# A seven-product MLP with one ring for its operands, some inner features stored in two parts, and transposes between its steps

## Chip, cores, metric

The kernel runs on one core of a Trainium2 chip. The metric is the device time of one execution in microseconds. Lower is better. Engines: TensorE (PE), VectorE (DVE), ScalarE (ACT), GpSimd (POOL) and SyncE (SP), which here only issues transfers. Transfers are also issued from ACT's and POOL's queues.

## The reference

Two blocks over 1024 tokens of width 1024, in float32. The first mixes by pooling, sparse attention and a short convolution, adds to the residual, and ends with a gated MLP; the second has spatial gating, window attention and attention to a memory of 256 rows. What matters here:

```
h  = h + m @ w_o
hn = rms_norm(h, norm2_g)
gate, up = split(hn @ w_gate_up)            # 1024 -> 2 x 2816
h  = h + (silu(gate) * up) @ w_down         # 2816 -> 1024
x  = rms_norm(h, final_g)                   # then the second block:
mkv = rms_norm(mem, mem_norm_g) @ w_mem_kv  # needs mem alone
bias = rel_bias[buckets]                    # a table for the window attention
```

## The kernel before

Every float32 product is made from three products of parts: an operand is split into hi (rounded, by an ACT copy) and lo (the rest, by a subtraction on POOL or DVE), and `mm3` (L283 to L285) issues hi x hi, hi x lo and lo x hi. So each operand costs two splits before TensorE can use it. Engines run their instructions in the order of the program text, each its own queue; `Side` objects insert small pieces of other work as TensorE advances (`tick` counts TensorE time, a generator yields the price of each piece).

The stages that the change touches, in order of time:

- **wb** (878 to 997 us). `proj_t` multiplies attention output by w_b, 16 outputs of 24 matmuls, each worth 8 x 0.64 us of ticks. For each output POOL issues loads of `g1d` and `mpart` (`load_gp`, L1062, L1063, two pairs of buffers), DVE multiplies and adds (L1078, L1079), ACT copies the hi part to `mh` (L1080), POOL subtracts the lo part. Two sides run: `mem_steps` (load a row of memory on POOL's queue, sum of squares, norm, transposes; two rows of tiles through one buffer) and `bias_steps` (32 small operations on POOL into `G`, then a transfer that writes `G`, 4 partitions x 384, 128 times each into the DRAM tile `gd`, issued from POOL).
- **wo** (997 to 1130 us). `mem_kv` (two passes of 48 matmuls), then the residual rows: `add_rows` for four column groups j of w_o and eight row tiles t. For j = 2 and 3 the loop goes over t: rows j = 2, rows j = 3, transposes of tile t - 2 (`first_turns`), and `norm2(t)`: two sums of squares on ACT, stores to `hres` on SP, reciprocal root and scaling on DVE, and for t >= 4 two differences of half tiles, one on POOL and one on DVE.
- **mlp** (1130 to 1605 us). The 2x2 block products are made with seven multiplications instead of eight. `gu_seq` lists the steps: a unit is 128-wide gate or up columns of a pair, seven products p each; a step is `gu_mm` (four `mm3` of 512 columns) and `gu_out` (eviction and block sums). For the first two units the products come in another order, because the transposed operands `TM[p]` are still being made by `turns(p)` (`turn4`: four transposes into one of two `ax` banks, ACT copies hi, DVE subtracts lo). `gu_prep` splits the weights of a step up to six steps ahead into `wpart` tiles (a ring of 8). After each pair `hidden_sums` makes four sums on POOL and seven 256 KB stores to `hd` follow behind the next `gu_mm`. `hb` tiles are a ring of 19.
- **down** (1605 to 1845 us). 77 steps m (seven products x 11 pairs): `dn_load` (one or two pieces of w_down into `rb`, one of `hd` into `ra`, rings of 8), `dn_sum`, `dn_hi` (two ACT copies), `dn_lo` (two DVE subtractions), then four `mm3`. `dn_ahead(m)` runs loads 7, sums 4, hi 3 and lo 2 steps ahead. The pool of these tiles opens when the pool of `TM[3..7]` closes, after the last `gu_mm`. The residual `h` is read back by eight 512 KB loads on ACT's queue at the start. The last products run beside `final_steps` (norms of finished tiles).

## Time and profile before

| what | value |
|---|---|
| median of three runs | 2282.96 us (2282.51, 2282.96, 2289.36) |
| profiled execution | 2287.99 us, span 2286.2 us |
| PE busy | 2178.9 us, 95% |
| PEld busy | 1879.6 us, 82% |
| DVE busy | 1349.0 us, 59% |
| POOL busy | 835.4 us, 37% |
| ACT busy | 786.4 us, 34% |
| granted TensorE clock, mean | 0.982 |
| DMA | 210.54 MB, 92 GB/s |

TensorE is busy nearly all the time, so what is to be read is where it is not: its waits, and the windows in which its clock is below full. A matmul's duration in a row is longer than its distance from the next one, because matmuls are pipelined; prices are taken from counts in a window of known length.

### The profile page before, as it was taken

To read this page: it belongs to the slowest core of one execution; us is meant where nothing else is said; L and a number is where in the kernel's file an instruction comes from. 1 tells how busy PE (TensorE), PEld (TensorE's weight loads), DVE (VectorE), ACT (ScalarE), POOL (GpSimd) and SP (SyncE) were. 2 spreads that over 40 slices of the span, in tenths; PEclk is the share of its full clock that TensorE was granted. 3 is DMA by queue.
4 is the path that set the end of the run, shared out by engine and by line. 5 is a ranking of instruction groups with operands and counts; after the bars stand their busy time and mean duration, and the time that the engine had idled before them with its cause. 6 is when DMAs were issued, how large, how long until landed. Compare 5 with 4: busy or idle time off the path is not lost. (4 is left out here: it accounts for less than half of the span.)

```text
span 2286.2 us, 31336 instructions
## 1 busy us (share of the span) xinstructions
PE 2178.9 (95%) x11855; PEld 1879.6 (82%) x11855; DVE 1349.0 (59%) x2712; ACT 786.4 (34%) x1548; POOL 835.4 (37%) x714
## 2 busy tenths in 40 slices
PE   7999999999999998969879999999799999999998
PEld 7789889998888887759858888888588789987998
DVE  6688998888892886411745333333477760831724
ACT  4573211121123875211233323222344532322631
POOL 1213322224533212633138777685100112671121
PEclk9999999999999999989989999999899999999999
DMA  4212222113321001335202323231976422120013
GB/s 144 70 65 75 65 74 65 56 38 111 115 70 38 1 1 56 121 82 167 97 26 87 114 92 116 92 116 51 341 280 207 171 75 70 47 65 19 1 62 142
DMA packets 144359, 210.54 MB, mean 92 GB/s; under 512 B 14768, under 2 KB 93332, under 8 KB 144208
## 3 DMA queue, kind: packets, MB, share of 16 engines
q1 hardware_dynamic: 127120, 162.55, 21.5%
q0 software_dynamic: 8800, 27.54, 3.5%
q10 hardware_dynamic: 8288, 18.45, 2.1%
q8 instruction: 93, 1.52, 0.3%
q14 instruction: 58, 0.48, 0.1%
HBM read 161.80 MB, written 46.66 MB: 91 GB/s over the span
## 5 line engine op out<-in xcount | busy, mean ns | idle before, releaser
L97 POOL TENSOR_TENSOR wpart<-wraw,wpart 128x1024 fp32r<-128x1024 f32 (+1 forms) x108 | 261.6, 2442 | 532.9 <-ACT wpart L96 531.2
L285 PE MATMUL mm<-xh,wpart 128*128 128x512 f32 (+2 forms) x736 | 269.9, 367 | 0.0
L284 PE MATMUL mm<-xl,wpart 128*128 128x512 f32 (+2 forms) x736 | 269.5, 366 | 0.0
L283 PE MATMUL mm<-xh,wpart 128*128 128x512 f32 (+2 forms) x736 | 269.0, 365 | 0.0
L608 DVE MAX8 m<-scores 128x8 f32<-128x272 f32 (+6 forms) x224 | 188.8, 843 | 6.4 <-POOL scores L570 0.2
L610 DVE MATCH_REPLACE8 scores<-m,scores 128x272 f32<-128x272 f32 (+6 forms) x224 | 184.9, 826 | 0.0
L285 PE MATMUL mm<-th,wpart 128*128 128x512 f32 x440 | 175.9, 400 | 6.5 <-POOL wpart L312 6.5
L283 PE MATMUL mm<-th,wpart 128*128 128x512 f32 x440 | 175.5, 399 | 3.8 <-ACT wpart L1226 3.8
L284 PE MATMUL mm<-tl,wpart 128*128 128x512 f32 x440 | 175.2, 398 | 0.0
L96 ACT ACTIVATE wpart<-wraw 128x1024 fp32r<-128x1024 f32 (+1 forms) x110 | 111.5, 1048 | 151.4 <-issue 80.5
L284 PEld LDWEIGHTS mm<-xl,wpart 128*128 128x128 f32 x736 | 138.5, 188 | 20.5
L283 PEld LDWEIGHTS mm<-xh,wpart 128*128 128x128 f32 x736 | 138.3, 188 | 20.3
L285 PEld LDWEIGHTS mm<-xh,wpart 128*128 128x128 f32 x736 | 138.3, 188 | 19.6
L283 PE MATMUL mm<-wpart,hh 128*128 128x256 f32 x512 | 142.7, 279 | 1.3 <-ACT ev L1717 1.3
L284 PE MATMUL mm<-wpart,hh 128*128 128x256 f32 x512 | 142.5, 278 | 0.0
L285 PE MATMUL mm<-wpart,hl 128*128 128x256 f32 x512 | 142.3, 278 | 0.0
L312 POOL TENSOR_TENSOR wpart<-hb,wpart 128x512 fp32r<-128x512 f32 x88 | 116.7, 1330 | 60.3 <-ACT wpart L1226 39.2
L283 PE MATMUL mm<-wpart,pa 128*128 128x512 f32 x242 | 97.0, 401 | 15.1 <-ACT pa L1417 15.1
L285 PEld LDWEIGHTS mm<-th,wpart 128*128 128x128 f32 x440 | 83.6, 190 | 27.8 <-POOL wpart L312 7.8
L283 PEld LDWEIGHTS mm<-th,wpart 128*128 128x128 f32 x440 | 83.4, 189 | 24.6 <-ACT wpart L1226 5.1
L284 PE MATMUL mm<-wpart,pa 128*128 128x512 f32 x242 | 97.6, 403 | 5.5 <-DVE wpart L312 5.5
L284 PEld LDWEIGHTS mm<-tl,wpart 128*128 128x128 f32 x440 | 83.4, 190 | 20.1
(382 smaller groups left out, 5716.4 us busy)
## 6 DMA issues: line engine op xcount, KB each, us to landing
wraw<-in_w_in_dram SPq DMA_DIRECT2D x68, 512.0 KB, 3.6
rb<-in_w_down_dram SPq DMA_DIRECT2D x99, 256.0 KB, 5.4
wraw<-in_w_gate_up_dram SPq DMA_DIRECT2D x44, 512.0 KB, 4.1
hd<-hb SPq DMA_DIRECT2D x77, 256.0 KB, 2.0
ra<-hd SPq DMA_DIRECT2D x77, 256.0 KB, 4.8
mpart<-ev POOLq DMA_DIRECT2D x32, 256.0 KB, 2.3
ev<-mpart POOLq DMA_DIRECT2D x32, 256.0 KB, 4.0
xr<-in_x_dram SPq DMA_DIRECT2D x8, 512.0 KB, 5.9
```

Source lines behind the costliest of these rows:

```text
L96: nc.scalar.activation(hi[:, :nk * w], r, AF.Copy)
L97: (low or nc.gpsimd).tensor_tensor(lo[:, :nk * w], r, hi[:, :nk * w].bitcast(F32), op=ALU.subtract)
L283: nc.tensor.matmul(o, sh, mh, start=start, stop=False, skip_group_check=more)
L284: nc.tensor.matmul(o, sh, ml, start=False, stop=False, skip_group_check=more)
L285: nc.tensor.matmul(o, sl, mh, start=False, stop=stop, skip_group_check=more)
L312: (eng or nc.gpsimd).tensor_tensor(out_lo, src, hi.bitcast(F32), op=ALU.subtract)
L608: nc.vector.max(m8, s)
L610: nc.vector.match_replace(out=s, in_to_replace=m8, in_values=s, imm_value=TAKEN)
```

## The change

The diff changes five places:

1. `bias_steps` yields less per step and 8 more at its end, and issues the `gd` transfer from ACT. `mem_steps` yields 30 (first) and 10 (second) after its row's load instead of 8.
2. `norm2` becomes `norm2_a` (sums of squares, stores) and `norm2_b` (the rest); the loop over t runs rows j = 2 of tile t + 1 ahead of `norm2_b(t - 1)` and rows j = 3 of tile t. `gu_sums(0)`, the first preps and the load of unit 1 move up in that loop.
3. `TM[3..7]` take ten tiles of one ring `tm`, whose slots the down steps use afterwards: a pair of steps takes one tile for `rb` and one for `pa`. The ring stays open through down, so a load may start when its slot's `TM` is no longer read. Loads run 8 steps ahead. For products with two weight pieces, `ra` is half a `wraw` tile. `h` is loaded in 16 pieces of 256 KB at the odd steps up to 7 of the first four products.
4. For products p = 4, 6 and 3 the inner features are stored as hi and lo parts (`SPLIT`): one more ACT copy and DVE subtraction in mlp, a second 256 KB store, 512 KB instead of 256 KB to load, and one split less in down. Stores are spread over the four steps after a pair.
5. The first units run in another order: each `mm3` of the first six steps is followed by one `turn4`. `W.ahead` at the end of down is emitted three steps earlier.

```diff
-                yield 1.5
-        nc.gpsimd.dma_start(gd, G.unsqueeze(1).to_broadcast([4, 128, 384]))
+                yield 1.2
+        yield 8.0
+        nc.scalar.dma_start(gd, G.unsqueeze(1).to_broadcast([4, 128, 384]))
...
-            yield 8.0
+            yield 30.0 if r == 0 else 10.0
...
+    add_rows(mh, ml, wo[2], 0, 2)
     for t in range(NT):
-        add_rows(mh, ml, wo[2], t, 2)
-        if t == 6:
-            gu_sums(0)
-        if t == 7:
-            for n in range(3):
-                gu_prep(n)
+        if t + 1 < NT:
+            add_rows(mh, ml, wo[2], t + 1, 2)
+        if t:
+            norm2_b(t - 1)
         add_rows(mh, ml, wo[3], t, 3)
+        if t < 7:
+            norm2_a(t)
         if 2 <= t < 6:
             first_turns(t - 2)
-        norm2(t)
+        if t == 4:
+            gu_sums(0)
+        if t == 6:
+            gu_prep(0)
+            gu_prep(1)
+            gu_load(1)
+        if t == 7:
+            gu_prep(2)
+    norm2_a(7)
...
+    def tm_tile():
+        return tmp_.tile([128, 2048], F32R, name="tm", bufs=10)
...
+    SPLIT = (4, 6, 3)
...
     def store(p, pr, t):
-        later.append(lambda: nc.sync.dma_start(hd[p - 1, pr], t))
+        if p not in SPLIT:
+            nc.sync.dma_start(hd[p - 1, pr, :, :512], t)
+            return
+        hi = hb_tile().bitcast(F32R)
+        nc.scalar.activation(hi, t, AF.Copy)
+        lo_of(t.bitcast(F32R), t, hi, nc.vector)
+        nc.sync.dma_start(hd[p - 1, pr, :, :512], hi.bitcast(F32))
+        nc.sync.dma_start(hd[p - 1, pr, :, 512:], t)
...
-        for p, t in ((1, a11), (2, a12), (4, a22), (7, s3), (5, a21), (6, s2), (3, s4)):
-            store(p, pr, t)
+        for k, (p, t) in enumerate(((1, a11), (2, a12), (4, a22), (7, s3), (5, a21), (6, s2),
+                                    (3, s4))):
+            at(n + 1 + k // 2, lambda p=p, t=t: store(p, pr, t))
...
             mm3(o, hi[:, k, :], lo[:, k, :], th[:, k, :], tl[:, k, :], first and k == 0, k == 3, not first)
-        for f in later:
-            f()
-        later.clear()
+            if extra:
+                turns(*extra.pop(0))
...
+        if m % 2 == 0:
+            DN["rb"], DN["pa"] = tm_tile(), tm_tile()
+            DN["ra"] = None
+        rb, pa = (DN[k][:, 1024 * (m % 2):1024 * (m % 2) + 1024] for k in ("rb", "pa"))
+        ra = rb[:, 512:]
+        if len(parts) == 2:
+            if DN["ra"] is None:
+                DN["ra"] = W.raw_tile()
+            ra = DN["ra"][:, 512 * (m % 2):512 * (m % 2) + 512].bitcast(F32R)
...
+        if p in SPLIT:
+            nc.sync.dma_start(pa.bitcast(F32), hd[p - 1, i])
+        else:
+            nc.sync.dma_start(ra.bitcast(F32), hd[p - 1, i, :, :512])
...
-        dn_load(m + 7)
+        dn_load(m + 8)
         dn_sum(m + 4)
         dn_hi(m + 3)
         dn_lo(m + 2)
...
+    norm2_b(7)
     gu_prep(3)
+    gu_prep(4)
+    gu_mm(0, [(5, t) for t in range(3)])
+    gu_out(0)
+    gu_mm(1, [(3, t) for t in range(3)])
+    sums24(range(3))
+    gu_sums(1)
+    gu_prep(5)
+    gu_mm(2, [(7, 0), (7, 1), (7, 2), (5, 3)])
+    gu_out(2)
+    gu_mm(3, [(3, 3), (7, 3), (6, 0), (6, 1)])
+    sums24((3,))
+    gu_out(1)
+    gu_out(3)
     gu_prep(6)
     gu_prep(7)
+    gu_mm(4, [(6, 2), (4, 0), (4, 1), (4, 2)])
+    gu_out(4)
+    gu_prep(8)
+    gu_prep(9)
+    gu_mm(5, [(6, 3), (4, 3)])
+    gu_out(5)
...
-    close(tmp_)
     dn_open()
     for n in (last - 1, last):
         gu_out(n)
-    for f in later:
-        f()
-    later.clear()
+    run_todo(last + 9)
...
-    for t in (4, 5, 6, 7, 0, 1, 2, 3):
-        nc.scalar.dma_start(h[:, t, :], hres[t])
+    h_load = [(t, c) for ts, c in ((range(4, 8), 1), (range(4), 0), (range(4, 8), 0), (range(4), 1))
+              for t in ts]
...
+        if i in (1, 3, 5, 7) and h_load:
+            t, c = h_load.pop(0)
+            nc.scalar.dma_start(h[:, t, 512 * c:512 * c + 512], hres[t, :, 512 * c:512 * c + 512])
+        if p == 3 and i == NPAIR - TAIL - 1:
+            W.ahead()
```

## Rows read from the trace of the kernel before

**Rows 1.** The page, part 2: TensorE's granted clock in tenths, 40 slices
```profile
PEclk9999999999999999989989999999899999999999
```

**Rows 2.** Windows: length, busy PE PEld DVE ACT POOL (xcount), clock, DMA share, GB/s
```profile
980.00:1000.00 20.00, 17.78 (x77) 13.94 (x75) 0.00 (x0) 0.00 (x0) 0.00 (x0) 1.00 0.24 26
1060.00:1080.00 20.00, 20.00 (x172) 20.00 (x172) 2.97 (x7) 0.01 (x1) 3.30 (x2) 1.00 0.17 54
1240.00:1260.00 20.00, 20.00 (x88) 16.13 (x87) 11.80 (x13) 5.21 (x9) 16.88 (x13) 1.00 0.31 105
1660.00:1680.00 20.00, 20.00 (x89) 16.43 (x88) 14.49 (x24) 8.40 (x15) 0.00 (x0) 1.00 1.04 382
```

**Rows 3.** Timeline of PE, transposes: start us, us, engine, line, operation, count
```profile
1152.06 1.03 PE L1145 MATMUL ax<-ident,hb 128*128 128x128 f32 x8
```

**Rows 4.** Waits of PE, whole span: us in total, times, longest us
```profile
PE mm L283 <- ACT wpart L96: 16.5, 2, 9.5
PE mm L283 <- ACT pa L1417: 15.1, 2, 10.8
PE mm L285 <- POOL wpart L312: 11.2, 4, 5.2
...
PE mm L1044 <- DVE mrow L1038: 9.4, 2, 8.9
```

**Rows 5.** Windows round the five stretches, columns as in rows 2
```profile
909.00:931.00 22.00, 13.15 (x50) 10.33 (x49) 9.04 (x24) 5.81 (x13) 9.92 (x21) 0.77 0.42 148
997.00:1036.10 39.10, 18.02 (x101) 16.75 (x100) 6.79 (x10) 9.87 (x14) 24.46 (x17) 0.69 0.37 123
1130.40:1200.30 69.90, 47.79 (x191) 35.06 (x189) 33.99 (x58) 23.18 (x43) 26.35 (x18) 0.83 0.15 48
1605.00:1632.00 27.00, 11.85 (x43) 8.67 (x42) 8.36 (x11) 5.84 (x11) 8.54 (x6) 0.79 0.95 352
1805.50:1845.40 39.90, 34.06 (x134) 25.37 (x134) 35.37 (x58) 17.80 (x32) 10.39 (x4) 0.96 0.26 92
```

**Rows 6.** Timelines of POOL, DVE and ACT at the end of wb
```profile
967.77 1.14 POOL L1026 DMA_DIRECT2D gd<-G  x1 [0.30 <-POOL G L1022]
...
1001.68 0.69 DVE L1078 TENSOR_TENSOR ev<-mm,ev 128x512 f32<-128x512 f32 x1 [30.39 <-DMA ev<-g1d]
...
1022.10 0.69 DVE L1078 TENSOR_TENSOR ev<-mm,ev 128x512 f32<-128x512 f32 x1 [4.09 <-DMA ev<-g1d]
...
1024.22 1.99 ACT L96 ACTIVATE wpart<-wraw 128x1024 fp32r<-128x1024 f32 x2
...
1025.62 9.36 POOL L97 TENSOR_TENSOR wpart<-wraw,wpart 128x1024 fp32r<-128x1024 f32 x4
```

**Rows 7.** DMA issues: count, KB each, median us from issue to landing
```profile
gd<-G POOLq DMA_DIRECT2D x1, 768.0 KB, 33.2
```

**Rows 8.** Timeline of DVE at the start of mlp
```profile
1137.17 0.74 DVE L1139 TENSOR_TENSOR hb<-mm,hb 128x256 f32<-128x256 f32 x2
...
1144.17 0.69 DVE L1173 TENSOR_TENSOR hb<-hb 128x512 f32<-128x512 f32 x1 [1.17 <-POOL hb L1172]
...
1158.57 4.67 DVE L1449 TENSOR_TENSOR hb<-hb 128x512 f32<-128x512 f32 x4
```

**Rows 9.** Timelines of SP, ACT and POOL between mlp and down
```profile
1605.74 0.33 SPq L1386 DMA_DIRECT2D rb<-in_w_down_dram  x1
...
1612.96 16.75 ACTq L1495 DMA_DIRECT2D hh<-hres  x8
...
1613.70 3.01 POOL L1291 TENSOR_TENSOR hb<-ev,hb 128x512 f32<-128x512 f32 x2 [11.47 <-DVE ev L1290]
...
1621.21 1.26 POOL L1303 TENSOR_TENSOR hb<-hb 128x512 f32<-128x512 f32 x1
```

**Rows 10.** Timeline of DVE at the end of down
```profile
1823.31 1.28 DVE L329 SCALAR_TENSOR_TENSOR hh<-hh,ry,pg 128x1024 f32<-128x1024 f32 x1
...
1829.31 3.42 DVE L329 SCALAR_TENSOR_TENSOR hh<-hh,ry,pg 128x1024 f32<-128x1024 f32 x1
```

More of the change, by code (lines that the diff above doesn't have):

```diff
@@ L1158, in build, with norm2_a, norm2_b @@
     TM = {}
-    def norm2(t):
-        ss = [work.tile([128, 4], F32, name="ss", bufs=4)[:, :1] for _ in range(2)]
+    ssq = {}
+    def norm2_a(t):
+        ssq[t] = [work.tile([128, 4], F32, name="ss", bufs=4)[:, :1] for _ in range(2)]
         for c in range(2):
-            sumsq(ht[t, c], ss[c])
+            sumsq(ht[t, c], ssq[t][c])
             nc.sync.dma_start(hres[t, :, 512 * c:512 * c + 512], ht[t, c])
-        nc.vector.tensor_tensor(ss[0], ss[0], ss[1], op=ALU.add)
-        y = rstd_b(rstd_a(ss[0]))
+    def norm2_b(t):
+        s0, s1 = ssq.pop(t)
+        nc.vector.tensor_tensor(s0, s0, s1, op=ALU.add)
+        y = rstd_b(rstd_a(s0))
         for c in range(2):
@@ L1337, in gu_out @@
             if u:
-                hidden_sums(u)
+                hidden_sums(u, n)
         elif p == 6:
@@ L1364, in gu_step, with turns @@
         gu_out(n)
-    def turns(p, ts=range(4)):
-        for t in ts:
-            turn4(ht[{5: (t, 0), 7: (t + 4, 0), 3: (t + 4, 1), 6: (t + 4, 1), 4: (t, 1)}[p]],
-                  *TM[p], 128 * t)
+    def turns(p, t):
+        turn4(ht[{5: (t, 0), 7: (t + 4, 0), 3: (t + 4, 1), 6: (t + 4, 1), 4: (t, 1)}[p]],
+              *TM[p], 128 * t)
     DN = {}
@@ L1414, in dn_hi @@
             return
-        dn_ops[m] = (W.part_tile(), DN["p"].tile([128, 1024], F32R, name="pa", bufs=6))
-        for o, src in zip(dn_ops[m], dn_src(m)):
-            nc.scalar.activation(o[:, :512], src, AF.Copy)
+        dn_ops[m] = W.part_tile()
+        nc.scalar.activation(dn_ops[m][:, :512], dn_src(m), AF.Copy)
+        if dn_seq[m][0] not in SPLIT:
+            rb, ra, pa = dn_raw[m]
+            nc.scalar.activation(pa[:, :512], ra.bitcast(F32), AF.Copy)
     def dn_lo(m):
@@ L1421, in dn_lo @@
             return
-        for o, src in zip(dn_ops[m], dn_src(m)):
-            lo_of(o[:, 512:], src, o[:, :512], nc.vector)
+        lo_of(dn_ops[m][:, 512:], dn_src(m), dn_ops[m][:, :512], nc.vector)
+        if dn_seq[m][0] not in SPLIT:
+            rb, ra, pa = dn_raw[m]
+            lo_of(pa[:, 512:], ra.bitcast(F32), pa[:, :512], nc.vector)
     def dn_ahead(m):
-        dn_load(m + 7)
+        dn_load(m + 8)
         dn_sum(m + 4)
@@ L1432, in dn_open @@
     def dn_open():
-        DN["p"] = pool("dn", side="left")
-        for m in range(7):
+        for m in range(8):
             dn_load(m)
@@ L1439, in dn_open, with sums24 @@
                 dn_lo(m)
[L1441 to L1451 removed]
+    def sums24(ts):
+        for t in ts:
+            nc.vector.tensor_tensor(ht[t + 4, 1], ht[t + 4, 1], ht[t, 0], op=ALU.subtract)
+            nc.gpsimd.tensor_tensor(ht[t, 1], ht[t, 1], ht[t + 4, 1], op=ALU.subtract)
+    norm2_b(7)
+    gu_prep(3)
+    gu_prep(4)
[9 more added lines that the diff above has]
+    sums24((3,))
     gu_out(1)
     gu_out(3)
[L1454 to L1459 removed]
     gu_prep(6)
     gu_prep(7)
[L1462 to L1469 removed]
+    gu_mm(4, [(6, 2), (4, 0), (4, 1), (4, 2)])
[4 more added lines that the diff above has]
+    gu_out(5)
+    ahead = 10
     last = len(gu_seq) - 1
[L1471 removed]
+    for n in range(6, last - 1):
         while ahead <= min(n + 6, last):
@@ L1574, in build @@
                     dn_ops.pop(g)
+                    dn_raw.pop(g)
             if len(grp) > 1:
@@ L1581, in build @@
     fa = Side(final_steps(range(4)))
-    W.ahead()
     MARK("fin")
     close(ttp)
-    close(DN["p"])
+    close(tmp_)
     yp = pool("y", side="left")
```

67 lines of the change are left out of this document (23 added, 44 removed).

## The prediction

> **What bounds the kernel now.** Four views, in this order. The page's line of granted clock, which is full except for a few slices [rows 1]; so time is lost in a few places, not everywhere. The windows of the unchanged bulk: TensorE is busy for all of 20 us, with 88 matmuls of 512 columns or 172 of 256 [rows 2]; this gives my prices, 20/88 = 0.227 us and 20/172 = 0.116 us at the 2.4 GHz level. A turn of four 128-column transposes costs 1.03/2 = 0.52 us [rows 3]. In such stretches only fewer matmuls would help, and the change removes none. Third, TensorE's waits: the long ones are for halves of weights, for a row of memory and for the first down operands [rows 4]. Fourth, windows round these waits [rows 5]: the five stretches in which TensorE is slower than its price, all touched by the change. What each loses is its length less its matmuls at the price (counts from the code, near the recorded ones):
>
> - wb, first memory row: 42 matmuls and 8 transposes are 10.6 us of 22.0: 11.4 lost.
> - end of wb and mem_kv: 96 at 0.116 and 5 at 0.227 are 12.3 of 39.1: 26.8 lost.
> - start of mlp: nine gu steps of 12 matmuls and 20 turns are 24.5 + 10.4 = 34.9 of 69.9: 35.0 lost.
> - mlp to down: 43 are 9.8 of 27.0: 17.2 lost.
> - end of down: 132 are 30.0 of 39.9: 9.9 lost.
>
> Together 100.3 us, waits and low clock both (granted 0.69 to 0.96 there, a mixture of 1.2 and 2.4 GHz [rows 5]). The question is how much of it stays.
>
> **wb, memory row.** Today the sum of squares is emitted 8 us of ticks after the row's load, but POOL and ACT reach load and use late, and TensorE's transposes stand 8.9 us behind the norm [rows 4]. With 30 the load is far ahead; the row's other steps keep their distances. Ticks per wb are 16 x 8 x 0.64 = 82 us, the memory steps now end at 60, so the drain in wo still has nothing to do. The second row keeps a distance of 10, and its transposes waited 0.5 us before (9.4 in two waits, less 8.9). Left: 1 us, from 0 to 3. Gain 10.4.
>
> **gd on the ACT queue.** Today POOL issues gd at 967.77, it takes 33.2 us to land at about 25 GB/s, and the g1d loads queued on POOL behind it land behind it: DVE waits 30.39 us for one, until 1001.68 [rows 6, 7]. Behind DVE stand ACT's mh copies, behind these the mkv splits, behind these TensorE. Afterwards gd is issued at 32 x 1.2 + 1 + 8 = 47 of 82 us of ticks, some 37 us ahead of wb's last matmul, and should have landed by then. What remains after that matmul: from DVE's eviction at 1022.10 to POOL's first lo half at 1025.62 it was 3.5 us, the mh copy and ACT's hi halves among it, and a lo half is 9.36/4 = 2.34 [rows 6]. So the lo halves of the second mkv pair are there at +5.8 and +8.2; TensorE has 48 x 0.116 = 5.6 us of first-pair matmuls, then 12 x 0.116, and loses about 1.2 us. On top I take 4 us because the g1d loads share transfer engines with gd for those 33 us. Left: 5, between 1 and 27 (nothing gained). Gain 21.8. The DMA engines' share during gd was 0.24 with almost nothing else moving [rows 2], about four of sixteen. The Trainium skill (DMA: Bandwidth & Descriptors, "Why a DMA increments its semaphore by 16 and not by 1") says that a transfer is spread over the largest number up to 16 that divides the slowest dimension, four here whichever queue issues it; the trace agrees, 0.24 against 4/16. By "Queues, rings and completion order" there, an engine changes queue only between packets: moving gd off POOL's queue shares these four engines, it doesn't free them. That speaks for my 4 us and for rival A.
>
> **Norms in two steps, turns between steps.** In wo, norms of tile t now follow the wo[2] rows of t + 1; TensorE had no gap there before and gets none. gu_load(1) moves up SP's queue ahead of the last two hres stores, whose readers come only in down; prep(2) then stands before the last norm on POOL, which ends the 5.2 us wait for a lo half [rows 4]. At the end of wo (time 0) DVE still has, in its queue ahead of every turn eviction, the last add (0.4), after ACT's sum the norm, and the difference behind POOL's: from 1137.17 to the end of 1144.17's 0.69 that was 7.7 us [rows 8]. So gu step 0 issues two turns into the two ax banks, stops at 2.9 us, and goes on at about 8.7: 5.8 us, part of the next step at half clock. After step 1, three differences (1.17 each, from 4.67 for 4) and three gu_sums stand ahead of the next evictions on DVE, some 8 us: TensorE stops again for about 5.3. A table load, Silu and two preps on ACT after step 3 cost about 2. Adding steps (6 x 2.72), turns (20 x 0.52) and these waits with the slow matmuls behind them I get 42.4 us to the end of step 5, then three steps of 2.72: 50.6 against 69.9. Left: 15.7, gain 19.3. Bounds: 8 left if POOL and DVE don't slow each other (a 128x512 difference is 0.69 alone, 1.17 beside POOL [rows 8]), 24 if each wait is half as long again. The Trainium skill (SBUF, "Who interferes with whom") has one exclusive port pair for these two engines; the trace agrees, 1.17 against 0.69, and without it the left-over would be near 8.
>
> **Parts stored, one ring.** Per pair: three hb tiles, three ACT copies, three DVE lo's more in mlp, 6 us of ACT and DVE work in 39 us in which each is busy under 60% (11.80 and 5.21 of 20 [rows 2]). The hb ring of 19 turns with 16 allocations per pair instead of 13; going round it, every tile's store is issued at least four steps before its slot is wanted. ACT may wait for POOL's sums, but splits are six steps ahead (16 us). Cost 0. If that cover were gone, a wait of 1 us per pair is 11 us.
> In down, SPLIT products need one ACT and one DVE operation less per step, and 256 KB more of load.
>
> **mlp to down.** Today SP's first down load goes out at 1605.74, when the tm pool closes; then eight 512 KB h loads hold ACT's queue from 1612.96 for 16.75 us, and the next hi halves stand behind them [rows 4, 9]. Afterwards slots come free as each TM's last step ends (up to 14 us earlier), the first three hi's are ready, and h comes in 16 pieces. New is what the last pair's parts put in: a DVE lo waits for POOL's s4, and dn_lo(2) is queued behind it. POOL's two products and four sums took from 1613.70 to 1622.47 [rows 9]; with one product left at the end, s4 is ready at about +7.4, dn_lo(2) is done at about +9.5, and TensorE wants it at +5.7. Left: 3.9 and 2 of slow clock, 6 (2 to 12). Gain 11.2.
>
> **End of down.** DVE is the bound there (35.37 busy of 39.9 [rows 5]). Eleven lo's of 0.68 go, 7.5 us. W.ahead is emitted three steps earlier, but ACT already runs its splits right behind the last hi, and POOL's lo's meet DVE as before (a norm of 3.42 instead of 1.28 [rows 10]). Left 2.5 (0 to 6), gain 7.4.
>
> **Sum.** 10.4 + 21.8 + 19.3 + 11.2 + 7.4 = 70.1. The profiled execution took 2287.99 us, 5 above the median of the three runs (2282.96), so it would be 2218 in this execution's terms and 2213 as a median. I say 2212. Bounds of the parts together: 2185 to 2255; all ends at once are unlikely, the forecast's own range is 2200 to 2222.
>
> **Rivals.** A: gd holds ACT. An issue that can't be taken in blocks its engine, as the h loads did: 16.75 us for eight [rows 9]. gd is 512 pieces on four engines, and the second memory row's sum of squares is queued behind it on ACT. If ACT stands for 16 us, TensorE stops for about 16 - 6 = 10 at that row's transposes, which are emitted 6 us of ticks after the sum: 2222; if for the whole 33.2, 27: 2239. For it: the 0.24 share. Against: POOL issued the same transfer in 1.14 [rows 6]. B: the turns hardly stall, 8 left instead of 15.7, and the other residues at their low ends: 2196. C: the first down loads don't leave early, because SP stands at an earlier store or gate load: 2223. D, the slower end: down becomes bound by its loads. 209 operand pieces of 256 KB, 4.2 MB of h, the last stores and z weights are 63 MB in 77 x 2.72 = 210 us, 300 GB/s. The trace has carried 382 GB/s with TensorE full [rows 2]. For it: loads now leave in pairs behind TensorE's release, and ra of two-part products behind dn_lo, in one SP queue. From 226 GB/s down (63 MB in 280 us) all 70 us are given back; at 210 the stage takes 300 us, 90 more, and the time is 2302. E: a cancelling mixture, or reordered code that doesn't act: 2280.
>
> **Chances.** Forecast 0.60, A 0.20, B 0.08, C 0.06, E 0.02, D 0.04. A measurement of this kernel tells about 0.3% (7 us) from no change. Faster 0.94 (forecast, A, B, C), same 0.02, slower 0.04. The range runs from B's side to the far end of A: 2192 to 2238.
>
> **What the profile after would show.** No wait of mm on mrow above 1 us; no DVE wait near 30 us for g1d; between the last wo matmul and step 6 about 42 us, with two TensorE waits of 5 to 6 us for tl; TensorE's wait at the start of down for a DVE wpart (dn_lo(2)), not for pa; DVE below 85% in the last product; 300 GB/s at most in down with TensorE full. Wrong would be: a long ACTq row of gd, waits for rb or pa inside down, or waits in the steady gu steps.

## The result, and the profile of the changed kernel

The changed kernel takes 2259.99 us (median of 4 runs, 2258.33 to 2262.50) where the kernel before takes 2284.66 (4 runs, 2282.51 to 2289.36): a ratio of 0.989, 95% interval 0.987 to 0.9911. That is 25 us, 1.1%, faster. (The two executions of the table below are 29.6 us apart, since that of before was 3 us above its median and that of after 2 below.) The forecast was 2212, a gain of 71, with a range of 2192 to 2238: the sign was right, the size a third of what I said, and the time lies outside the range.

Where the gain went shows in one table. It cuts both profiled executions (spans 2286.2 and 2256.6 us) at TensorE's first and last matmul of each stage, read from the timelines, and sets the forecast beside it.

| Stretch | before | after | gain | forecast |
|---|---|---|---|---|
| wb, first to last matmul | 105.7 | 101.3 | 4.4 | 10.4 |
| last wb to first wo matmul (mem_kv) | 38.7 | 21.2 | 17.5 | 21.8 |
| wo | 94.3 | 93.8 | 0.4 | 0 |
| last wo matmul to end of gate/up step 8 | 69.9 | 70.5 | -0.6 | 19.3 |
| step 8 to last gate/up matmul | 405.1 | 412.1 | -7.0 | 0 |
| last gate/up to last down matmul | 239.8 | 226.4 | 13.3 | 18.6 |
| after down | 441.1 | 439.5 | 1.6 | 0 |

The line of granted clock, which answers to [rows 1], keeps one dip, at the start of mlp (slices 20 and 21 of 40); those at the end of wb and at the start of down are gone:

```profile
PEclk9999999999999999999889999999999999999999
```

TensorE's waits (us in total, times, longest) answer to [rows 4]. Those for pa and for POOL's wpart L312 are gone, and those for ACT's wpart L96 have fallen from 16.5 to 5.4 us, but there is a new list of single waits of 4 to 10 us. The waits for tm are the turns' waits for their lo halves; in the kernel before they were six short ones for tl, shown first. The wait for ev L1392 has no counterpart before.

```profile
PE ax L1145 <- DVE tl L1149: 5.7, 6, 1.0
```

```profile
PE ax L1146 <- DVE tm L1150: 18.6, 3, 10.3
...
PE mm L284 <- DVE wpart L312: 9.8, 3, 4.3
PE mm L1045 <- DVE mrow L1039: 7.2, 2, 5.4
PE mm L283 <- ACT wpart L1233: 6.3, 1, 6.3
PE mm L283 <- ACT wpart L96: 5.4, 1, 5.4
PE mm L283 <- DVE ev L1392: 5.4, 1, 5.4
```

Windows round these waits (length, busy PE, PEld, DVE, ACT, POOL with counts, granted clock, DMA share, GB/s) answer to [rows 5]; the fourth is a new loss in the gate/up steps, where before TensorE was full.

```profile
931.00:943.00 12.00, 6.55 (x24) 5.07 (x23) 7.23 (x18) 2.62 (x6) 10.48 (x20) 0.72 0.40 144
993.00:1014.20 21.20, 13.67 (x99) 13.11 (x98) 4.49 (x6) 6.83 (x10) 15.24 (x11) 0.84 0.44 148
1108.00:1178.50 70.50, 43.62 (x191) 33.87 (x190) 42.31 (x72) 25.28 (x47) 30.97 (x22) 0.78 0.16 48
1200.00:1220.00 20.00, 14.64 (x57) 11.46 (x56) 10.08 (x12) 5.72 (x10) 17.32 (x12) 0.91 0.50 172
1590.60:1612.00 21.40, 17.13 (x68) 13.44 (x67) 11.17 (x18) 9.52 (x17) 9.07 (x8) 0.92 0.76 261
1777.50:1817.40 39.90, 34.35 (x138) 27.23 (x137) 30.26 (x50) 13.12 (x23) 8.82 (x4) 0.91 0.38 132
```

The long waits are gone, but behind most of them the next thing was late too. The experiments take the new waits one by one, by stage. All change the changed kernel, not the kernel before; their ratios are to the kernel before on the same chip. The changed kernel was run again beside some of them:

> The changed kernel as it is, on the same chip as the three before, to measure them against it. Expected: 2255 to 2265 us, ratio to the kernel before 0.987 to 0.991, and stretches within 1 us of those of its first trace.

It measured 2260.30 us, ratio 0.9882 (0.9861 to 0.9903), with the stretches up to the last down matmul within 0.9 us of the first trace and the part after down 3.2 us longer, where I expected 1 at most. A single edit of 2 to 5 us is within the intervals of such ratios, so the stretches of the traces carry the small ones. Each stretch is read from one execution, and it varies where no edit touches it: between the runs here wb from 100.9 to 104.2 us, the gap behind it from 18.8 to 22.0 (the two together from 121.9 to 123.9), the start of mlp from 70.5 to 71.7, the gate/up steps from 412.0 to 413.2.

### The profile page after: what moved, and what is told of

The parts are those of the page before. It is cut to its first block, busy times and chain, and to the rows that moved or that the text cites. A ratio compares the mean times of both kernels' runs of the same rounds, so it can differ in the third digit from the quotient of the medians.

```text
span 2256.6 us, 31373 instructions
## 1 busy us (share of the span) xinstructions
PE 2166.0 (96%) x11855; PEld 1872.9 (83%) x11855; DVE 1382.1 (61%) x2712; ACT 785.9 (35%) x1548; POOL 840.0 (37%) x713
## 4 chain that ended last, share of the span: by engine, by line
PE 84%; issue 4%; DVE 4%; DMA 3%; POOL 3%; ACT 2%; ACTq 0%; DVEq 0%; SPq 0%; POOLq 0%
PE mm L285 24%; PE mm L284 24%; PE mm L283 24%; PE ax L283 2%; PE ax L285 2%; PE ax L284 2%; PE mm L956 1%; PE ax L1928 1%; DMA ev<-mpart 1%; PE mm L1870 1%; POOL wpart L97 1%; PE mm L337 1%; DMA ev<-g1d 1%; DVE scores L565 1%; PE mm L1906 1%
## 5 line engine op out<-in xcount | busy, mean ns | idle before, releaser
L97 POOL TENSOR_TENSOR wpart<-wraw,wpart 128x1024 fp32r<-128x1024 f32 (+1 forms) x108 | 259.4, 2420 | 531.1 <-ACT wpart L96 510.9
L283 PE MATMUL mm<-tm,wpart 128*128 128x512 f32 x440 | 175.2, 398 | 5.4 <-DVE ev L1392 5.4
L285 PE MATMUL mm<-tm,wpart 128*128 128x512 f32 x440 | 174.4, 396 | 0.0
L284 PE MATMUL mm<-tm,wpart 128*128 128x512 f32 x440 | 174.3, 396 | 0.0
L96 ACT ACTIVATE wpart<-wraw 128x1024 fp32r<-128x1024 f32 (+1 forms) x110 | 111.5, 1048 | 150.7 <-issue 80.5
L312 POOL TENSOR_TENSOR wpart<-hb,wpart 128x512 fp32r<-128x512 f32 x88 | 119.0, 1360 | 36.0 <-ACT wpart L1233 36.0
L284 PE MATMUL mm<-wpart,tm 128*128 128x512 f32 x242 | 97.1, 401 | 9.8 <-DVE wpart L312 9.8
L283 PEld LDWEIGHTS mm<-tm,wpart 128*128 128x128 f32 x440 | 83.0, 189 | 25.2 <-DVE ev L1392 5.8
L285 PEld LDWEIGHTS mm<-tm,wpart 128*128 128x128 f32 x440 | 83.0, 189 | 20.0
L284 PEld LDWEIGHTS mm<-tm,wpart 128*128 128x128 f32 x440 | 83.1, 189 | 19.8
L312 POOL TENSOR_TENSOR wpart<-wraw,wpart 128x512 fp32r<-128x512 f32 x66 | 90.0, 1371 | 19.8 <-ACT wpart L1233 19.7
```

The lines of the kernel that those rows point to most:

```text
L96: nc.scalar.activation(hi[:, :nk * w], r, AF.Copy)
L97: (low or nc.gpsimd).tensor_tensor(lo[:, :nk * w], r, hi[:, :nk * w].bitcast(F32), op=ALU.subtract)
L283: nc.tensor.matmul(o, sh, mh, start=start, stop=False, skip_group_check=more)
L284: nc.tensor.matmul(o, sh, ml, start=False, stop=False, skip_group_check=more)
L285: nc.tensor.matmul(o, sl, mh, start=False, stop=stop, skip_group_check=more)
L312: (eng or nc.gpsimd).tensor_tensor(out_lo, src, hi.bitcast(F32), op=ALU.subtract)
```

## Experiments: the start of mlp

In the changed kernel the end of wo looks like this on DVE (start, length, line, operation, idle time before with what ended it). Behind the last wo matmul at 1108.02, the sum of tile 7 (L1140) ends at 1122.75, because norm2_b(5), which has just begun, the sum of tile 6 and norm2_b(6) with its difference stand ahead of it; norm2_b(7) follows, and the first turn's tl (L1150) begins at 1129.93.

```profile
1107.55 0.15 DVE L1173 TENSOR_TENSOR ss<-ss 128x1 f32<-128x1 f32 x1
...
1112.82 0.42 DVE L1140 TENSOR_TENSOR hb<-mm,hb 128x256 f32<-128x256 f32 x1
1114.08 0.16 DVE L1173 TENSOR_TENSOR ss<-ss 128x1 f32<-128x1 f32 x1 [0.85 <-ACT junk L316]
...
1122.34 0.41 DVE L1140 TENSOR_TENSOR hb<-mm,hb 128x256 f32<-128x256 f32 x1
...
1128.27 1.73 DVE L1180 TENSOR_TENSOR hb<-hb 128x512 f32<-128x512 f32 x1 [1.15 <-POOL hb L1179]
1129.93 1.27 DVE L1150 TENSOR_TENSOR tm<-ax,tm 128x512 fp32r<-128x512 f32 x2
```

TensorE meanwhile (same columns) begins gate/up 6.6 us late, since ACT's squares of tile 6 wait for DVE and the first hi halves for ACT; then it waits for that tl:

```profile
1114.62 0.80 PE L283 MATMUL mm<-tb,wpart 128*128 128x512 f32 x1 [6.32 <-ACT wpart L1233]
...
1130.75 0.66 PE L1146 MATMUL ax<-ident,hb 128*128 128x128 f32 x2 [10.27 <-DVE tm L1150]
```

**The sums ahead of the norm.**

```diff
-        if t:
-            norm2_b(t - 1)
         add_rows(mh, ml, wo[3], t, 3)
         if t < 7:
             norm2_a(t)
+        if t:
+            norm2_b(t - 1)
```

> The changed kernel with one order turned round: in wo's last loop the sums of wo[3] for tile t and their squares are emitted ahead of norm2_b(t - 1), not behind it. Theory (DVE's queue in wo's tail makes the late start of mlp): in the changed kernel DVE added tile 7 at 1122.34, 14.3 us behind the last wo matmul at 1108.0, because the norm of tile 6 with its difference (1114.08 to 1122.4) stood ahead of it; the sum then falls to about 1.5 us behind that matmul, the square of tile 6 no longer holds ACT's first gate/up halves, so the first gate/up matmul comes at +2 to +3 instead of +6.6, the first tl of (5,0) at about +12 instead of +22, and the stretch from the last wo matmul to the end of step 8 shrinks from 70.5 to about 61. Time about 2250, 10 us below the changed kernel's 2260. Rival (the order is a symptom: DVE and POOL have too much work between them at that place, in whatever order): the norms come later instead, the stretch stays within 3 us of 70.5 and the time within 2257 to 2263.

Measured: 2258.77 us, ratio 0.9866 (0.9853 to 0.9880). The sum of tile 7 came 5.5 us behind the last wo matmul instead of 14.3, and gate/up began at 0.6 instead of 6.6, but the first tl came at 19.2 instead of 21.9, and the stretch is 67.3 us, between the two expectations. The reason is in DVE's timeline: the norms of tiles 5, 6 and 7 now stand in a row, from 1106.6 to 1126.6, 6.7 us each. At that pace DVE falls behind TensorE, which finishes a tile of wo in 5.6 us (48 matmuls at 0.116).

**Both differences on DVE**, besides.

```diff
-            nc.gpsimd.tensor_tensor(a, b, a, op=ALU.subtract)
+            nc.vector.tensor_tensor(a, b, a, op=ALU.subtract)
```

> The first experiment (sums of wo[3] ahead of the norm of the tile before), and both half-tile differences of norm2_b on DVE. Theory (a late norm takes DVE 7.2 us, of which 1.15 are a wait for POOL's difference and 1.05 the slowing of its own by POOL's lo halves; so three norms in a row hold the first turns' evictions 6 us longer than they need): a norm takes DVE 5 to 5.5 us, the first tl comes at about +14 from the last wo matmul and not +19, and the stretch to the end of step 8 falls from the first experiment's 67.3 to about 62; time 4 to 6 us below that run's. Rival (POOL and DVE don't matter to each other here, the number of instructions in the queue does): the stretch stays within 1.5 us of 67.

Measured: 2257.41 us, ratio 0.9867 (0.9847 to 0.9888), stretch 66.9, where the rival had it. My theory fell: the first tl came 18.1 us behind the last wo matmul, and I expected 14. The rival's reason (POOL and DVE don't matter to each other here) doesn't hold either. The wait for POOL's difference is gone, but POOL's lo halves (L312) come earlier now, and the 128x1 steps of the norm meet them: a pair of 0.22 and 0.16 us takes 2.35.

```profile
1107.72 0.16 DVE L278 SCALAR_TENSOR_TENSOR ry<-rt,ry 128x1 f32<-128x1 f32 x1
1107.92 1.14 DVE L274 SCALAR_TENSOR_TENSOR rt<-ry,rv 128x1 f32<-128x1 f32 x1
1109.10 1.21 DVE L278 SCALAR_TENSOR_TENSOR ry<-rt,ry 128x1 f32<-128x1 f32 x1
...
1107.77 2.52 POOL L312 TENSOR_TENSOR wpart<-wraw,wpart 128x512 fp32r<-128x512 f32 x2 [44.08 <-ACT wpart L1233]
```

**Another order of the opening**, with both edits above: no turn in step 0, norm2_b(7) behind two turns, the sums between turns. Short lines are joined in this and the later cuts of the opening.

```diff
-    norm2_b(7)
     gu_prep(3); gu_prep(4)
-    gu_mm(0, [(5, t) for t in range(3)]); gu_out(0)
-    gu_mm(1, [(3, t) for t in range(3)])
-    sums24(range(3)); gu_sums(1); gu_prep(5)
+    gu_mm(0); gu_out(0)
+    gu_mm(1, [(5, 0), (5, 1)]); norm2_b(7)
+    gu_mm(2, [(3, 0), (3, 1), (5, 2)]); gu_out(2); sums24((0, 1))
+    gu_mm(3, [(3, 2), (5, 3), (3, 3)]); sums24((2,)); gu_sums(1); gu_prep(5)
...
```

> The changed kernel with the sums of wo[3] ahead of the norm of the tile before (as in the first experiment), both half-tile differences of norm2_b on DVE, and another order at the start of mlp: no turn in gate/up step 0, the norm of tile 7 behind step 1 with two turns, the other turns two to four a step up to step 7, sums24 and gu_sums(1) spread between steps 2 and 5. Theory (TensorE waits 10.3 and 6.3 us for tl because DVE still has three norms, then three sums24 and three gu_sums, in its queue ahead of the turns' evictions; the first experiment took only the sums out of that queue): the norm of tile 6 ends at about +9 from the last wo matmul and not +20, the first turns' tl at about +11, the two long waits become waits below 4 us each, and the stretch from the last wo matmul to the end of step 8 falls from 70.5 to between 55 and 60. Time 11 to 15 us below the changed kernel's. Rival (ACT and the gate/up loads are as late as DVE, so that the waits change their names): 65 to 68 for the stretch, about what the first experiment gave, with TensorE waiting for wpart.

Measured: 2247.86 us, ratio 0.9823 (0.9805 to 0.9841). The stretch is 57.4 us, 9.5 less than with the two edits alone, as the theory had it: what a turn waits for is its place in DVE's queue. (Of the 12 us in the time, 2.4 lie in wo, whose matmuls ran at another pace in this execution; the last section has this.) The waits for tl shrink from 18.6 us to 7.3:

```profile
PE ax L1146 <- DVE tm L1150: 7.3, 3, 2.9
PE mm L283 <- ACT ev L1369: 5.8, 2, 5.1
```

**The two edits apart.** The change itself made two edits here, and undoing one at a time separates them: first wo's last loop alone as it was before (the whole norm of tile t behind its own sums; `gu_sums(0)`, the first preps and the load of unit 1 go back with it), then the opening alone.

```diff
     for t in range(NT):
+        add_rows(mh, ml, wo[2], t, 2)
...
         add_rows(mh, ml, wo[3], t, 3)
         if 2 <= t < 6:
             first_turns(t - 2)
+        norm2_a(t)
+        norm2_b(t)
...
-    norm2_a(7)
...
-    norm2_b(7)
     gu_prep(3)
```

> The changed kernel with wo's last loop as it was before the change (the norm of tile t whole, right behind its own sums, the first gate/up halves at t = 7), and with the new opening of mlp. Theory (norms in two steps made the tail of wo later: in the kernel before, the norm of tile 7 with its difference ended 14.5 us behind the last wo matmul, in the changed one 21.9, since each norm stands ahead of the next tile's sum): the norm of tile 7 ends at +14 to +16, TensorE's first wait for tl is 3 to 5 us and not 10.3, the stretch from the last wo matmul to the end of step 8 falls from 70.5 to 63 to 66, and the time by 5 to 7 us against the changed kernel. Rival (the loop's order doesn't matter, the new opening has too much on DVE by itself): the stretch stays within 2 us of 70.5.

```diff
+    norm2_b(7); gu_step(0); gu_mm(1)
+    turns_all(5, (0, 1, 2)); gu_prep(3); gu_step(2)
+    turns_all(5, (3,)); turns_all(3); sums24(range(4)); gu_mm(3)
...
```

> The changed kernel with wo's last loop as changed, and with the opening of mlp as it was before the change (turns in blocks of three and four between whole gate/up steps, sums24 for all four tiles at once). Theory (the interleaving does save: a turn in a block takes 1.0 us, since its two banks wait for the evictions, and 0.36 to 0.52 between groups of matmuls, about 10 us for twenty turns; the later norms of the new loop ate this gain): the stretch from the last wo matmul to the end of step 8 grows from 70.5 to 77 to 82, and the time by 7 to 11 us against the changed kernel. Rival (interleaving saves nothing, DVE's work sets the length in either order): 69 to 72.

Measured: with the old loop 2253.95 us, ratio 0.9855 (0.9836 to 0.9875); with the old opening 2264.24, ratio 0.9891 (0.9873 to 0.9910). The stretches make a square:

| | old opening | new opening |
|---|---|---|
| old loop | 69.9 | 63.4 |
| new loop | 74.2 | 70.5 |

Interleaving the turns saves 6.5 us with the old loop and 3.7 with the new one, where I expected 6.5 to 11.5 with the new one; the new loop costs 4.3 and 7.1 us. The two edits cancelled. What the new loop's parts cost singly, norms in two steps and the moved sums, preps and load, these runs don't separate; the timelines put it down to the norms. With the old loop the waits for tl are 13.3 us in all, and norm2_b(7) ends 15.8 us behind the last wo matmul instead of 22.0:

```profile
PE ax L1146 <- DVE tm L1150: 13.3, 3, 6.3
```

## Experiments: gate/up steps and down

The first pair's sums end on POOL at 1207.94, since its last step brings four blocks at once. DVE's lo halves of the stored parts (L312) wait for them, an eviction (L1392) stands behind these, and TensorE behind it:

```profile
1204.73 0.69 DVE L312 TENSOR_TENSOR hb<-hb 128x512 fp32r<-128x512 f32 x1 [2.55 <-POOL hb L1339]
...
1207.97 3.41 DVE L312 TENSOR_TENSOR hb<-hb 128x512 fp32r<-128x512 f32 x2 [1.95 <-POOL hb L1341]
1211.31 0.68 DVE L1392 TENSOR_TENSOR ev<-mm,ev 128x512 f32<-128x512 f32 x1
```

**No parts at all**, and **parts for pairs 1 to 9 alone.**

```diff
-    SPLIT = (4, 6, 3)
+    SPLIT = ()
```

> The changed kernel with SPLIT empty: no product's inner features are stored in parts, everything else is kept. Theory (stored parts cost the 7 us that the steady gate/up steps grew by, through the first pair, and TensorE's wait at the start of down): the stretch from step 8 to the last gate/up matmul falls from 412.1 to about 405, the 5.4 us wait of TensorE behind DVE's eviction of product 5 goes, the 4.3 us wait for the second down operand goes; against it 33 more lo halves of 0.68 us on DVE in down, 7.5 us of them in the last product, where DVE was the bound in the kernel before: last product 4 to 8 us longer. Time about 2256, 2252 to 2261. Rival (the 7 us come from the ring of ten tiles or the stores' new places, not from parts): the stretch stays near 412, down's end gets longer, 2262 to 2268.

In store, dn_load, dn_hi and dn_lo alike:

```diff
+    def in_parts(p, pr):
+        return p in SPLIT and 0 < pr < NPAIR - 1
-        if p not in SPLIT:
+        if not in_parts(p, pr):
```

> The changed kernel with parts stored for pairs 1 to 9 alone: the first and the last of the eleven pairs of blocks are stored whole. Theory (only where POOL's sums of a pair are late does a lo half on DVE stall the queue: first pair, whose last product brings four blocks at once, and last pair, behind which down's operands stand): the stretch from step 8 to the last gate/up matmul falls from 412.1 to about 405, TensorE's wait at the start of down falls from 4.3 to under 1.5, the end of down stays within 2 us. Time about 2250. Rival (the first pair that is stored in parts always stalls, whichever it is, because ring or queues have to settle): the 5.4 us wait moves to the second pair and the stretch stays within 2 us of 412; time about 2256.

Measured: without parts 2255.33 us, ratio 0.9850 (0.9837 to 0.9864): the gate/up stretch is 405.0, and down 230.3 against 226.2. With parts for the middle pairs 2250.34, ratio 0.9841 (0.9826 to 0.9857): 405.0, and down 224.3. So the 7 us came from the first pair alone, no other pair takes its place, and TensorE is full, with 87 matmuls where 57 stood:

```profile
1200.00:1220.00 20.00, 20.00 (x87) 16.15 (x86) 11.63 (x10) 6.78 (x12) 19.77 (x15) 1.00 0.38 132
```

The parts do save what they were to save in down, 6 us (230.3 against 224.3). The wait at the start of down was to fall from 4.3 to under 1.5 us. It is gone, but waits of 2.3 and 0.5 us stand some 26 us into down instead, as in the run without parts (2.2 and 0.5).

**The end of down.** In the changed kernel a pair of norms takes 6.70 us on DVE while POOL makes the lo halves of W.ahead, and TensorE waits 4.2 us for the lo half behind it; a wait of 1.4 us, for the lo half ahead of the pair, comes before it. [rows 10] had the same meeting with 3.42 instead of 1.28.

```profile
1796.43 6.70 DVE L329 SCALAR_TENSOR_TENSOR hh<-hh,ry,pg 128x1024 f32<-128x1024 f32 x2
...
1795.84 2.93 POOL L97 TENSOR_TENSOR wpart<-wraw,wpart 128x1024 fp32r<-128x1024 f32 x1 [14.73 <-ACT wpart L96]
1799.50 2.55 POOL L97 TENSOR_TENSOR wpart<-wraw,wpart 128x1024 fp32r<-128x1024 f32 x1 [0.73 <-PE mm L285]
```

```diff
         if p == 3 and i == NPAIR - TAIL - 1:
-            W.ahead()
+            W.split_to(W.nu + W.AHEAD, nc.vector)
+            W.load_to(W.nu + W.LOADS)
```

> The changed kernel with the lo halves of the weights that W.ahead splits near the end of down on DVE, not on POOL; place and order are kept. Theory (the two waits of TensorE there, 1.4 and 4.2 us for a lo half, come from DVE losing 4.2 us of a norm while POOL works on its two 128x1024 differences): DVE spends about 2 x 1.3 us of its own in place of them, the norm pair takes 2.5 us and not 6.7, the two waits fall from 5.5 to 2 to 4 us in all, down from its first to its last matmul from 226.2 to about 223.5, the time falls by 2 to 4 us. Rival (DVE has no room there, whoever does the differences): waits and stretch stay within 1 us.

Measured: 2255.97 us, ratio 0.9859 (0.9842 to 0.9876). The norm pair takes 2.48 us, the two lo halves 2.35 together on DVE, and down 220.5 instead of 226.2 us, 5.7 less, more than expected: the wait behind the pair fell from 4.2 to 0.9, the one ahead of it stayed at 1.4, and the clock in the last 39.9 us rose from 0.91 to 1.00.

```profile
1797.22 2.48 DVE L329 SCALAR_TENSOR_TENSOR hh<-hh,ry,pg 128x1024 f32<-128x1024 f32 x2
...
1772.60:1812.50 39.90, 37.65 (x164) 29.95 (x163) 32.10 (x57) 14.75 (x25) 7.20 (x4) 1.00 0.44 152
```

## Experiments: wb and mem_kv

The memory row now lands far ahead, yet TensorE waits 5.4 us for its norm. DVE's queue shows why: the norm (from 934.21) stands behind an eviction (L1079) that waits for g1d, and POOL issued this load (L1063) behind the weight splits (L97).

```profile
922.82 5.23 POOL L97 TENSOR_TENSOR wpart<-wraw,wpart 128x1024 fp32r<-128x1024 f32 x2
927.97 0.60 POOL L1063 DMA_DIRECT2D ev<-g1d  x1
...
932.60 0.69 DVE L1079 TENSOR_TENSOR ev<-mm,ev 128x512 f32<-128x512 f32 x1 [6.83 <-DMA ev<-g1d]
```

**The load ahead of the splits.**

```diff
         units = W.get("wb", 2)
+        load_gp()
         W.ahead()
...
-                load_gp()
+                if t0 or ct:
+                    load_gp()
```

> The changed kernel with the loads of g1d and mpart that belong to the first half of a wb group issued on POOL ahead of the group's weight splits (W.ahead), not behind them. Theory (TensorE's wait at the first memory row no longer comes from the row's load but from an eviction: DVE's norm at 934.21 stood behind an eviction that waited 6.8 us for g1d, whose load POOL issued at 927.97, behind two lo halves of 5.2 us): the load goes out 5 us earlier, the norm comes as much earlier, the 5.4 us wait on mrow falls below 1.5, and the stretch of wb from its first to its last matmul falls from 101.3 to about 95; the weights' lo halves come 1.2 us later, which costs nothing. Time 5 to 7 us below the changed kernel's. Rival (the g1d data are late for another reason, the POOL queue's own order or the transfer): the wait on mrow stays above 4, stretch and time stay within 2 us.

Measured: 2257.51 us, ratio 0.9865 (0.9847 to 0.9882). wb is 94.5 us, 6.8 less; no wait on mrow is above 1.2. But the gap to wo grew from 21.2 to 24.3, since the loads of wb's second half still land late: 3.1 of the gain were given back there, and the two stretches together gave 3.7 us, less than the 5 to 7 expected.

**gd on sixteen engines.** These late loads (15.4 us to land, median of three, between 955 and 987) run beside gd. The change moved gd to ACT's queue, where its issue takes 0.76 us; it still moves at about 25 GB/s where nothing else does, on a quarter of the engines, so I split it by heads.

```diff
-        nc.scalar.dma_start(gd, G.unsqueeze(1).to_broadcast([4, 128, 384]))
+        for h_ in range(4):
+            nc.scalar.dma_start(gd[h_:h_ + 1], G[h_:h_ + 1].unsqueeze(1).to_broadcast([1, 128, 384]))
```

> The changed kernel with the 768 KB of gd issued as four transfers, one per head, at the same place on ACT's queue, so that the slowest dimension is 128 rows and not 4 heads. Theory (gd goes over four DMA engines for 33 us and the g1d loads, spread over all, land late behind it: 12.7 us for one, with DVE waits of 7.3 and 6.9 us): gd is through in 8 to 12 us, the DMA share is above 0.8 meanwhile, later g1d loads land in 3 to 4 us, the last wb eviction follows the last wb matmul by 2 to 3 us instead of 8, and the gap between the last wb and the first wo matmul falls from 21.2 to about 15. Time about 2254. Rival (the late evictions come from POOL's queue, where lo halves and weight splits stand ahead of the issues of the loads): gap within 2 us of 21, 2258 to 2262.

Measured: 2268.63 us, ratio 0.9912 (0.9899 to 0.9926), slower than the changed kernel. Neither theory had this. The DMA share rises to 0.81, the pace stays at 26 GB/s, and the four issues hold ACT for 12.95 us, with the second row's squares behind them; TensorE waits 10.3 us at that row. wb is 9.4 us longer and the gap to wo 3.8 shorter, at 17.4; down is 3.1 us longer too, though the edit doesn't touch it: its matmuls ran at a slower pace in this execution.

```profile
954.71 12.95 ACTq L1028 DMA_DIRECT2D gd<-G  x4
...
PE mm L1046 <- DVE mrow L1040: 14.1, 2, 10.3
...
960.00:966.00 6.00, 2.42 (x11) 1.62 (x9) 0.33 (x1) 0.00 (x0) 0.00 (x0) 0.95 0.81 26
```

So the number of engines doesn't set the pace. What stayed the same is the source: each row of G lies in one partition and is read 128 times.

**gd later, from DRAM:** G's 6 KB go out at the old place, the copies in wo behind j = 1.

```diff
-        nc.scalar.dma_start(gd, G.unsqueeze(1).to_broadcast([4, 128, 384]))
+        nc.scalar.dma_start(gs, G)
...
+    nc.scalar.dma_start(gd, gs.unsqueeze(1).to_broadcast([4, 128, 384]))
```

> The changed kernel in which the ACT queue writes only G's 6 KB at the old place and copies them out 128 times per head into gd from DRAM to DRAM in wo, after its second group of weights. Theory (the 768 KB of gd on the engines slow the g1d loads in the second half of wb: waits of 7.3 and 6.9 us on DVE): those loads land in 4 to 5 us, the last eviction of wb follows its last matmul by 3 us instead of 8, the gap between the last wb and the first wo matmul falls from 21.2 to about 15, and wo stays at 93.8. Time 5 to 7 us below the changed kernel's. The transfer's own pace shows whether a single SBUF partition as its source set the 25 GB/s: with DRAM as the source it should then be above 50 GB/s. Rival (the order on POOL alone makes the loads late): the gap stays within 2 us of 21.

Measured: 2254.95 us, ratio 0.9852 (0.9831 to 0.9873). The gap to wo is 13.3 us instead of 21.2, wo stays at 93.8, and six g1d loads between 955 and 987 land in 4.0 us (median; the changed kernel's line stands first).

```profile
ev<-g1d POOLq DMA_DIRECT2D x3, 256.0 KB, 15.4
...
ev<-g1d POOLq DMA_DIRECT2D x6, 256.0 KB, 4.0
```

With DRAM as its source gd moves at some 100 GB/s on the same quarter of the engines; the DMA rows for 1052 to 1062 us, 40 slices, gd from the tenth slice on (a weight load stands on top in slices 22 to 31):

```profile
DMA  0000000002122222222224889999996222222222
GB/s 0 0 0 0 0 0 0 0 0 31 55 92 98 98 104 98 111 106 109 98 98 127 266 295 389 389 393 371 385 395 254 70 57 63 106 94 104 76 109 96
```

## Experiments: all together

> The changed kernel with the edits of five experiments together: parts stored for pairs 1 to 9 alone, g1d loads ahead of the splits in wb, gd copied out in wo from DRAM, the lo halves near the end of down on DVE, and the other order at the start of mlp. Theory (the causes are separate and lie one behind another on TensorE's path, so the gains add): from the stretches of the single runs wb 6.8, end of wb and mem_kv 7.8, start of mlp 13.1, steady gate/up 7.1, down 5.7 for its end and 1.9 for its start are 42.4 us less than the changed kernel: about 2218 as a median, 2213 to 2224. Rival (the two edits of wb relieve the same loads, and the wait behind the last eviction stays whatever comes first): 8 to 12 us of it are not had, 2226 to 2230.

Measured: 2218.29 us, ratio 0.9689 (0.9669 to 0.9709): 42.0 us below the changed kernel on the same chip, where the sum of the parts said 42.4. The rival fell: wb and the gap gave 15.0 together. So the causes are separate in the main. That the sum agrees to 0.4 us is luck: the start of mlp gave 15.9 us instead of 13.1, with nearly the same waits as in its own run (mean clock 0.87 instead of 0.82), and down 4.4 instead of 7.6. The stretches are 94.5 (wb), 12.9 (gap), 94.0 (wo), 54.6 (start of mlp), 405.0 and 221.8 (down). The waits that remain in these stages:

```profile
PE ax L1149 <- DVE tm L1153: 6.9, 3, 2.9
PE mm L283 <- ACT ev L1376: 5.7, 2, 5.0
PE mm L284 <- DVE wpart L312: 5.3, 3, 3.1
```

The second of them is ACT's copy of step 0, queued behind the squares of tile 7. One more run takes it out of the way (the cut is against the kernel of all five edits):

```diff
-    norm2_a(7)
...
-    gu_prep(3); gu_prep(4); gu_mm(0); gu_out(0)
+    gu_mm(0); gu_out(0); norm2_a(7); gu_prep(3); gu_prep(4)
```

> The kernel of all five edits, and besides at the start of mlp ACT copies the result of gate/up step 0 ahead of the squares of tile 7 and the halves of the fourth and fifth operand. Theory (in the run of the other order TensorE stood 5.1 us before step 1, which adds onto the bank that this copy reads, because the copy was queued on ACT behind the squares that wait for DVE's last sum): the wait falls below 1.5 us, the stretch from the last wo matmul to the end of step 8 from 57.4 to about 53, the time 3 to 5 us below the kernel of all five edits. Rival (the norm of tile 7 comes as much later as its squares, and the turns wait for it): the wait moves to tl, the stretch stays within 1.5 us.

Measured: 2217.12 us, ratio 0.9686 (0.9666 to 0.9707), not to be told from the run before; the stretch is 54.3. The rival held: the wait moved on to tl.

```profile
PE ax L1149 <- DVE tm L1153: 11.5, 4, 4.7
```

Both are faster than either kernel: 69 and 70 us below the kernel before.

## Why the prediction was wrong, step by step

**What bounds the kernel, and the prices.** Right: but for 2 us, every gain and loss lies in the five stretches and, new, at the first pair. The forecast failed in what stays of each stretch's loss.

**wb, memory row** (gain 10.4 forecast, 4.4 measured). The step "with 30 the load is far ahead; the row's other steps keep their distances" was right on the load and left out DVE (7.0 us are left, of 0 to 3 forecast): the norm is queued behind an eviction, and this one's load behind POOL's splits. Mending that gave 6.8 us; with the 4.4 that is 11.2, near the forecast.

**gd on the ACT queue** (21.8 forecast, 17.5 measured). Mechanism right: the 30 us wait is gone, and rival A is refuted, since the issue took 0.76 us. Left are 9 us instead of 5, because I took 4 us for shared engines, where the loads took 15 us each to land; gd's removal gave 7.8. The prediction took from the Trainium skill (DMA: Bandwidth & Descriptors, "Why a DMA increments its semaphore by 16 and not by 1") that gd runs on four engines, for a slowest dimension of four. On the share it agrees with the runs here (0.24, then 0.81 with 128 rows). My later step from there, that four engines make gd long, failed: it moved at 25 GB/s on four engines, 26 on sixteen, and about 100 on four with another source.

**Norms in two steps, turns between steps** (19.3 forecast, -0.6 measured; the main miss). The step that failed is "At the end of wo (time 0) DVE still has, in its queue ahead of every turn eviction, the last add (0.4), after ACT's sum the norm, and the difference behind POOL's". I took one norm's 7.7 us from [rows 8] and set their start to time 0. Already in the kernel before they start 6.85 us behind the last wo matmul (1130.32), because the norm of tile 6 begins only then:

```profile
1130.84 0.16 DVE L1166 TENSOR_TENSOR ss<-ss 128x1 f32<-128x1 f32 x1 [0.85 <-ACT junk L316]
```

In the new order three norms were left (tiles 5, 6 and 7), the last sum stood behind two of them, and the last difference ended at 22.0 us instead of the 7.7 forecast (14.5 in the kernel before). The forecast had TensorE start at 0, stop at 2.9 and go on at 8.7; it started at 6.6, stopped at 12.5 and went on at 22.7. Of the 19.9 us between the 50.6 forecast and 70.5, 6.6 are the late start, 4.5 the longer first wait (10.3 for 5.8), 1.0 the second (6.3 for 5.3), 2.0 a third that I hadn't, and the remaining 5.8 small waits and slow matmuls (0.78 is the window's mean clock). The square of four runs shows that the interleaving gives 3.7 to 6.5 us and the new loop takes 4.3 to 7.1.

**Parts stored, one ring** (0 forecast, -7.0 measured). I priced the lost cover, 1 us per pair, and named ACT as the engine that would wait for POOL's sums. It was DVE, with an eviction behind it, and in one pair, where POOL's three products and four sums come last; the other pairs cost nothing. The sum has no term for a first pair; waits in the steady gu steps were among the signs of being wrong that I named.

**mlp to down and the end of down** (18.6 forecast, 13.3 measured). The start was right: TensorE waits 4.3 us for dn_lo(2), and the 21.4 us window with 68 matmuls at 0.227 loses 6.0, as forecast. The end was not: 39.9 us with 138 matmuls lose 8.6, and 2.5 were forecast. "POOL's lo's meet DVE as before" was the wrong step. Before, one norm lost 2.1 us; moved three steps earlier, the splits met two norms, which lost 4.2. The Trainium skill (SBUF — State Buffer, "Who interferes with whom") has one port pair that DVE and GpSimd share, as an exclusive lock; 6.70 us less 2.48 beside 5.5 us of POOL agrees. With POOL out of it a window of the same length loses 2.7, near the 2.5 forecast. Rival D is refuted: TensorE was full at up to 401 GB/s over 20 us, above the 300 that I called the most, and TensorE waited for no load inside down. DVE was busy for 76% of the last product, under the 85 that I named.

**Sum and range.** Three of five terms (wb, the start of mlp, the end of down) had a second queue behind the wait that I removed, a fourth the late loads, and I gave each residue as if these were independent and small. Three residues lie above the bounds that I gave them: 7.0 us of at most 3, 35.6 of 24, 8.6 of 6. In the stretches the misses add up: 6.0 + 4.3 + 19.9 + 7.0 + 5.3, less 2.0 gained in wo and after down, are 40.5, the difference between the 70.1 forecast and the 29.6 of the two executions. The kernel of all edits lands at 2217, near the forecast. That is not the forecast come true: it took further edits, and its start of mlp is 3.7 us above the forecast (54.3 for 50.6), its gap behind wb 4.0 below (12.9 for 16.9). It shows that losses of this size were there to be had, and that the change's order of instructions didn't get them.

## What to carry to other kernels

When a change takes a long wait away, list what else is in the queue of the engine that was waited for, in emission order, and when each of these can start: the time is that of the last, and at the start of mlp it was later than what had been removed. An operation cut in two and moved behind another tile's work must be followed on its own engine: it may have been in the right place. Look at the first and the last turn of a loop by themselves, as the steady part says nothing of them.

## What the runs showed of the hardware

A broadcast of rows that lie in one SBUF partition each moved at 25 to 26 GB/s at a DMA share of 0.24 (one transfer of four rows) and of 0.81 (a transfer for each row), and at about 100 with the rows in DRAM; while it ran, other loads took 15.4 us instead of 4.0. Whether the single partition or another property of this source sets the pace was not taken further.

Stretches without waits are not always equally fast. The 40 us from 40 us behind down, at a granted clock of 1.00 in both, hold 356 matmuls in the first trace of the changed kernel, one every 0.113 us, and 342 in its second, one every 0.118 us:

```profile
1857.06:1897.06 40.00, 40.00 (x356) 40.00 (x355) 0.00 (x0) 11.07 (x20) 13.26 (x6) 1.00 0.25 74
...
1858.47:1898.47 40.00, 40.00 (x342) 40.00 (x341) 0.00 (x0) 11.10 (x21) 11.76 (x5) 1.00 0.24 73
```

The part after down takes 439.5 us in the one and 442.7 in the other, so the 1.6 us of the table's last line say nothing of the change. In the same way wo took 91.4 us in the run with another order of the opening and 93.8 to 94.3 in the others, the kernel of all five edits with the same order in wo among them (94.0), and down 229.3 us in the run with gd in four transfers and 226.1 to 227.0 in the others that don't change it. Why the pace differs stays open.
